# Bias-by-distance tiles: read back from DRAM rows written 128 times, in place of flips on TensorE

## Chip, cores and metric

The kernel runs on one core of a Trainium2 chip. The metric is the device time of one execution in microseconds. Before the change the median of three runs is 1805.74 us (1804.57 to 1810.54).

## The reference, cut to what matters

Two transformer blocks work one after the other on 256 tokens of width 1024. The first block has an attention over tokens and context (MLA), a Fourier mixer and a mixture of 32 experts. The second block has an "even" layer with two families of eight heads each (MoBA and NSA), an MLP, an "odd" layer with sixteen heads, and a second MLP. The change concerns the even layer alone, whose scores get a bias that depends on the head and on the distance of query and key:

```python
n = jnp.maximum(dist, 0)
large = 16 + (jnp.log(max(n, 1) / 16) / math.log(1024 / 16) * 16).astype(jnp.int32)
bucket = jnp.where(n < 16, n, jnp.minimum(large, 31))
s_own = einsum('hqd,hkd->hqk', q, k) * scale + rel_bias.T[:, bucket(t[:, None] - key[None, :])]
```

Keys after the query are masked. For each of the 16 heads the bias is therefore one row of numbers, a function of the distance, and the tile that the scores need is that row shifted by one place from each query to the next.

## The kernel before, in words

All large inputs come through one stream of chunks of at most 1 MB. `post_chunks`, `expert_chunks` and `pre_project` list them in the order of use. `Stream.pump` (line 152) issues the loads on SP's queue (line 164), in that order and as far ahead as ring buffers are free: ring A has 7 buffers, ring B 6, and rings C, D and E, opened one after the other before the experts, 3, 2 and 3. A job may carry other small loads behind its own (`also`, line 396). `Stream.prepare` (line 170) splits a chunk of float32 into a high and a low part (two ScalarE casts on line 1565, two VectorE subtractions on line 1566) in ring B, and `Stream.get` hands it to the matmuls.

Order of the stages: projections of the first block (`pre_project`), attention (`pre_attend`), output projection and routing (`pre_finish`), experts (`moe`), then `even`, `mlp`, `odd`, `mlp`. The output weights are four chunks ("o", in the order 3, 0, 1, 2; line 421) and right behind them in the stream come the expert weights, 384 chunks of 1 MB, and behind these the chunks of the second block.

The bias rows are made in these steps:

- `bias_rows_in` (line 1686) loads a table of 33 x 384 (a one-hot row per bucket, and the mask) on ScalarE's queue, at the end of `pre_attend`.
- `bias_rows` (line 1690) multiplies it by the 32 x 16 table of biases on TensorE, which gives 16 rows of 384 numbers, one per head. ScalarE evicts them with a factor of -1, and GpSimd's queue writes them to a DRAM tensor `scr` of 16 x 384. It runs in `pre_finish`, between two parts of the output projection.
- `bias_chunk2` (line 1699) adds two chunks to the stream, each of 1 MB: partition p of the chunk gets, for eight heads, the 256 numbers of the row from place p on. Two steps of one place, over partitions and over columns, can only shift in one direction, so the tile comes out with its queries upside down.
- `bias_tiles` (line 1706) turns it round: each chunk is split like a weight chunk and multiplied by a flipped unit matrix, in eight matmuls of 512 columns (four banks, high and low part), and ScalarE and VectorE evict the four banks in turn to the tile `bt[i]`.

`even_project` (line 1943) projects queries, keys and values in the order of the stream. The first tile is turned round after the second query chunk, ahead of the small matmul for the gates (line 2003); its bias is used first by the MoBA scores on line 1865. The second tile is turned round after the third pair of key chunks, ahead of the value projections; the NSA scores use it (line 2149). The small matmul for the gates needs its weights split by ScalarE and VectorE (`small_pair`, line 1821).

```python
for c in range(4):
    cols(w, 256 * c, None if c else self.split_first)
    if c == 1:
        self.bias_chunk2(0)
cols(w, 2048)
self.bias_chunk2(1)
```

Of the kernel before, what the change touches and what calls it, by code (L numbers as in the profile page):

```python
# [9 lines left out]
F32 = mybir.dt.float32  # L10
# [9 lines left out]
P = 128  # L20
D = 1024
KD = 8
T = 256
# [198 lines left out]
class Kernel:  # L222
# [142 lines left out]
    def pre_project(self, A, B):  # L365
# [8 lines left out]
        for nm, n in rows:  # L374
            src = I[nm]
            if len(src.shape) == 2:
# [21 lines left out]
                ("o", 3): self.expert_bias_in(B)}  # L398

        def add(nm, q, cols, f, split=None):  # L400
            st.add(cols, lambda v: f(v) + also.get((nm, q), []), 0, split)
# [62 lines left out]
        self.mrow = B.tile([P, 512], F32, name="mrow")  # L464
# [163 lines left out]
    def pre_attend(self, B, C):  # L628
# [66 lines left out]
        four_w()  # L695
        for h in range(6):
            b = self.bank()
            for k in range(2):
                self.mm3(b, [a[:, k, 256 * (h % 3) : 256 * (h % 3) + 128] for a in wkv[h // 3]], [a[:, k] for a in kvl], k == 0, k == 1)
            nc.vector.tensor_tensor(kn[:, h], b, rqk[:, 256:768], OP.mult)  # L700
            if h % 2 == 0:
                rope(qr[h // 2], 0, "q")
                split_rope(h // 2)
            if h in (2, 4):
                four_v(h // 2 - 1)
            self.modulation(MODS[h])
# [118 lines left out]
        self.bias_rows_in(B)  # L825
# [21 lines left out]
    def pre_finish(self, B, C, R):  # L847
# [15 lines left out]
        fills = [lambda: self.bcast_row(C, self.gc, g1b, bank="b"), router, lambda: self.bias_rows(B), lambda: self.down_bias_in(R),  # L863
# [730 lines left out]
    def post_chunks(self):  # L1594
# [21 lines left out]
        for c in range(4):  # L1616
            cols(w, 256 * c, None if c else self.split_first)
            if c == 1:
                self.bias_chunk2(0)
        cols(w, 2048)  # L1620
        self.bias_chunk2(1)
# [64 lines left out]
    def bias_rows_in(self, pool):  # L1686
        self.bk = pool.tile([E + 1, 384], F32, tag="mrow", name="bk")
        self.nc.scalar.dma_start(out=self.bk, in_=self.I["bucket"][0 : E + 1, 0:384])

    def bias_rows(self, pool):  # L1690

        nc, bk = self.nc, self.bk
        b = self.bank("bk", "s")
        nc.tensor.matmul(b[0:16, 0:384], self.rb, bk, start=True, stop=True)
        t = pool.tile([16, 384], F32, tag="krp", name="bkt")
        nc.scalar.mul(t, b[0:16, 0:384], -1.0)
        nc.gpsimd.dma_start(out=self.scr, in_=t)

    def bias_chunk2(self, i):

        def src(v):
            return [(v.rearrange("p (h c) -> p h c", h=8),
                     bass.AP(tensor=self.scr.tensor, offset=self.scr.offset + 8 * 384 * i, ap=[[1, P], [384, 8], [1, T]]))]
        self.stream.add((2048,), src, 0, self.split_plain)

    def bias_tiles(self, i, flip):

        nc = self.nc
        w = self.stream.get()
        for h in range(4):  # L1710
            b = self.bank("fl", "acc")
            for n in range(2):
                nc.tensor.matmul(b, flip, w[n][:, 512 * h : 512 * h + 512], start=(n == 0), stop=(n == 1))
            o = self.bt[i][:, 2 * h : 2 * h + 2].rearrange("p h c -> p (h c)")
            if h % 2:
                nc.vector.tensor_copy(o, b)
            else:
                nc.scalar.copy(o, b)
        self.stream.free()
# [223 lines left out]
    def even_project(self, W, X):  # L1943
# [4 lines left out]
        self.bt = [W.tile([P, 8, T], F32, tag=f"bt{i}", name="bt") for i in range(2)]  # L1948
        qk = W.tile([P, 16, T], F32, tag="qk", name="qk")
# [6 lines left out]
        flip = W.tile([P, 256], F32R, tag="hs1", name="flipr")[:, 0:P]  # L1956
        nc.scalar.copy(flip, self.c2("flip"))
# [42 lines left out]
        self.todo = []  # L2000
        self.bias_tiles(0, flip)
# [46 lines left out]
        self.bias_tiles(1, flip)  # L2048
# [393 lines left out]
def body(tc, I, out, dbg=None, upto=None):  # L2442
    nc = tc.nc
    K = Kernel(tc, I, dbg)
    with ExitStack() as es:
# [19 lines left out]
        K.scr = dr.tile([16, 384], F32, name="scr")[:]  # L2465
# [41 lines left out]
```

## Time and profile before

| What | Value |
|---|---|
| Median of three runs | 1805.74 us |
| The profiled execution | 1805.48 us |
| Its span, first to last instruction | 1803.7 us |
| TensorE busy | 1721.6 us (95%) |
| VectorE busy | 744.8 us (41%) |
| ScalarE busy | 583.3 us (32%) |
| Mean DMA rate over the span | 307 GB/s |
| Mean granted clock of TensorE | 0.996 |

The page cuts the span into 40 equal slices of 45.1 us. A busy share is an average over stages that have different limits, so the stages have to be looked at one by one: attention and routing end at some 200 us, the experts at some 1150 us, and the even layer follows. TensorE's busy time counts matmuls that overlap in the pipeline, and a busy TensorE need not be at its peak. DMA shares a little over 1 occur.

### The profile page before, as it was taken

The page shows a single profiled execution, that of the slowest core. Times are in us where ns is not written, and L with a number is a line of the kernel's source. Part 1 is how long each engine was busy: PE and PEld are TensorE (multiplying, and loading weights), DVE is VectorE, ACT ScalarE, POOL GpSimd, SP SyncE. Part 2 cuts the span into 40 slices and gives each one's busy share as a digit, 9 for nine tenths or more (in the row PEclk, how much of TensorE's full clock was granted, in tenths as well). Part 3 has the DMA queues.
Part 4 walks back from the last instruction along what each step waited for, and adds up shares of the span by engine and source line. Part 5 has one row for each costly group of instructions (what it writes and reads, how often), then busy time and mean ns, then how long its engine had stood idle before and what let it go on. Part 6 is the DMA issues. An engine that isn't in the chain of part 4 may idle for free.

```text
span 1803.7 us, 24461 instructions
## 1 busy us (share of the span) xinstructions
PE 1721.6 (95%) x9553; PEld 1031.0 (57%) x9553; DVE 744.8 (41%) x1604; ACT 583.3 (32%) x1147; POOL 22.8 (1%) x31
## 2 busy tenths in 40 slices
PE   8989999999999999999998998899999999999998
PEld 6756543333333333333332332588699989989997
DVE  4675522222221112212211112576665558756554
ACT  5534311111111111111111110555654446545444
POOL 0000000000000000000000000100000001000000
PEclk9999999999999999999999999999999999999999
DMA  9987899999999999999999999986165563345540
GB/s 351 327 278 278 322 386 410 411 412 412 412 412 411 411 412 412 413 412 411 411 412 413 413 413 412 312 241 189 48 210 187 187 186 129 131 139 196 185 147 24
DMA packets 202461, 553.45 MB, mean 307 GB/s; under 512 B 11136, under 2 KB 87430, under 8 KB 200294
## 3 DMA queue, kind: packets, MB, share of 16 engines
q1 hardware_dynamic: 201290, 550.35, 80.9%
q8 instruction: 76, 1.25, 0.3%
q0 software_dynamic: 576, 0.86, 0.2%
q10 hardware_dynamic: 476, 0.64, 0.1%
q14 instruction: 43, 0.35, 0.1%
HBM read 550.71 MB, written 1.07 MB: 306 GB/s over the span
## 4 chain that ended last, share of the span: by engine, by line
PE 72%; DMA 18%; DVE 6%; ACT 3%; issue 1%; SPq 0%; ACTq 0%; DVEq 0%
PE acc L1795 11%; PE g L1209 10%; PE u L1209 10%; PE ot L1780 10%; PE y L1220 8%; DMA ring<-in_w_gate 7%; DMA ring<-in_w_up 5%; DMA ring<-in_w_down 4%; PE pj L1780 4%; PE xg L1292 3%; PE pj L1787 2%; PE yb L1362 1%; PE bk L542 1%; PE mix L363 1%; DVE msum L314 1%
## 5 line engine op out<-in xcount | busy, mean ns | idle before, releaser
L1566 DVE TENSOR_TENSOR ring<-ring,ring 128x1024 fp32r<-128x1024 f32 (+1 forms) x200 | 234.3, 1215 | 77.8 <-ACT ring L1565 77.3
L1209 PE MATMUL g<-ring,xg 128*64 128x512 f32 x1056 | 254.9, 605 | 8.8 <-DMA ring<-in_w_gate 8.7
L1209 PE MATMUL u<-ring,xg 128*64 128x512 f32 x1056 | 248.2, 602 | 10.0 <-DMA ring<-in_w_up 9.2
L1220 PE MATMUL y<-ring,ht 128*64 128x512 f32 x1056 | 240.8, 598 | 16.2 <-DMA ring<-in_w_down 15.7
L1565 ACT CAST ring<-ring 128x1024 fp32r<-128x1024 f32 (+1 forms) x200 | 198.5, 1046 | 75.7 <-PE acc L1795 54.3
L1281 ACT ACTIVATE z<-y,gsl 64x512 fp32r<-64x512 f32 x66 | 45.0, 682 | 429.1 <-PE y L1220 402.1
L1780 PE MATMUL ot<-ahi,ring 128*128 128x256 f32 x960 | 177.2, 282 | 0.0
L1220 PEld LDWEIGHTS y<-ring,ht 128*64 128x64 f32 x1056 | 70.0, 136 | 164.7 <-issue 117.0
L1282 DVE SCALAR_TENSOR_TENSOR z<-y,gsl,z 64x512 fp32r<-64x512 f32 x66 | 49.5, 750 | 251.0 <-ACT z L1281 250.9
L1780 PEld LDWEIGHTS ot<-ahi,ring 128*128 128x128 f32 x960 | 151.3, 191 | 1.3
L1209 PEld LDWEIGHTS u<-ring,xg 128*64 128x64 f32 x1056 | 67.3, 136 | 131.9 <-issue 99.3
L1209 PEld LDWEIGHTS g<-ring,xg 128*64 128x64 f32 x1056 | 67.2, 137 | 128.6 <-issue 118.9
L1780 PE MATMUL ot<-alo,ring 128*128 128x256 f32 x480 | 135.6, 283 | 0.0
L1795 PE MATMUL acc<-ring,hhi 128*128 128x512 f32 x480 | 131.5, 395 | 0.0
L1795 PEld LDWEIGHTS acc<-ring,hhi 128*128 128x128 f32 x480 | 88.1, 188 | 19.0
L1228 ACT ACTIVATE sg<-gm 128x512 f32<-128x512 f32 x33 | 20.8, 630 | 239.5 <-DVE gm L1227 239.5
L1780 PEld LDWEIGHTS ot<-alo,ring 128*128 128x128 f32 x480 | 91.8, 191 | 1.3
L1294 ACT ACTIVATE xg<-xg,mod,a 128x128 f32<-128x128 f32 (+1 forms) x136 | 50.9, 452 | 99.2 <-PE xg L1292 99.2
L1292 PEld LDWEIGHTS xg<-pm,x 128*128 128x128 f32 x544 | 65.2, 195 | 26.8 <-issue 15.4
L1780 PE MATMUL pj<-ahi,ring 128*128 128x256 f32 x416 | 79.9, 287 | 0.0
L1271 DVE TENSOR_SCALAR gt<-gt,cp 128x256 fp32r<-128x256 f32 x33 | 16.0, 484 | 150.6 <-PE gt L1269 150.6
L1795 PE MATMUL acc<-ring,hlo 128*128 128x512 f32 x240 | 75.4, 395 | 0.0
(518 smaller groups left out, 2080.5 us busy)
## 6 DMA issues: line engine op xcount, KB each, us to landing
ring<-in_w_gate SPq DMA_DIRECT2D x128, 1024.0 KB, 17.9
ring<-in_w_up SPq DMA_DIRECT2D x128, 1024.0 KB, 17.9
ring<-in_w_down SPq DMA_DIRECT2D x128, 1024.0 KB, 17.9
ring<-in_mlp_w SPq DMA_DIRECT2D x64, 1024.0 KB, 5.4
ring<-in_w_mod SPq DMA_DIRECT2D x24, 1024.0 KB, 6.4
ring<-in_odd_w_in SPq DMA_DIRECT2D x12, 1024.0 KB, 5.3
ring<-in_even_w_in SPq DMA_DIRECT2D x7, 1024.0 KB
ring<-in_w_out SPq DMA_DIRECT2D x4, 1024.0 KB, 5.0
```

Source lines behind the costliest of these rows:

```text
L1209: nc.tensor.matmul(acc[64 * h : 64 * h + 64], xg[:, 2 * q + j], w[:, j, 512 * h : 512 * h + 512], start=(q == 0 and j == 0), stop=False, s ...
L1220: nc.tensor.matmul(acc[64 * h : 64 * h + 64], l, w[:, j, 512 * h : 512 * h + 512], start=(q == 0 and j == 0), stop=(q == 3 and j == 1), sk ...
L1228: nc.scalar.activation(sg, gm, AF.Sigmoid, scale=1.702)
L1281: nc.scalar.mul(t[s], a[s], g[s])
L1282: nc.vector.scalar_tensor_tensor(t[o], a[s], g[s], t[s].bitcast(F32), OP.mult, OP.subtract)
L1292: nc.tensor.matmul(b[:, n * j : n * j + n], self.x[:, t, (k + j) * P : (k + j + 1) * P], pm[:, t, 0:n], start=(t == 0), stop=(t == 1))
L1294: nc.scalar.activation(xg[:, k + j], b[:, n * j : n * j + n], AF.Identity, bias=self.mod[:, 0, 24 + k + j : 25 + k + j], scale=self.a2[:, ...
L1565: nc.scalar.copy(hi[:, c], v[:, c])
L1566: nc.vector.tensor_tensor(lo[:, c], v[:, c], hi[:, c].bitcast(F32), OP.subtract)
L1780: nc.tensor.matmul(out, w[a][:, k, c : c + n], x[b][:, k], start=(k == 0 and i == 0), stop=(k == KD - 1 and i == 2))
L1787: nc.tensor.matmul(out, x[a][:, k, t * P : (t + 1) * P], w[b][:, k, c : c + n], start=(k == 0 and i == 0), stop=(k == KD - 1 and i == 2))
L1795: nc.tensor.matmul(acc[2 * t + n], x[a][kx][:, t * P : (t + 1) * P], w[b][:, j, 512 * n : 512 * n + 512], start=(first and i == 0), stop=( ...
```

## The change

The row of each head is written to DRAM 128 times end to end (`scr` becomes 16 x 128 x 384). Read with a step of 383 from partition to partition, one less than the length of a row, it gives a tile whose rows shift the other way, so it comes out in the order that the scores want. The tile is read straight to `bt[i]`, in float32, with no split, no matmul and no eviction.

- The 33 x 384 table is loaded behind the second key/value chunk ("k", 1) on SP's queue. It lies in the buffer of `mrow`, which is allocated anew behind it.
- `bias_rows` runs in `pre_attend`, behind `four_w()`. Its result lies in a tile of its own, `bkt`.
- The two writes, heads 0 to 7 and heads 8 to 15, go on SP's queue with the job of output weights ("o", 1), the third of the four, behind its load.
- The two chunks of bias leave the stream.
- `bias_tiles(0)` issues its read on SP's queue at the start of `even_project`, `bias_tiles(1)` at the place where the second tile was turned round.

```diff
-                ("o", 3): self.expert_bias_in(B)}
+                ("k", 1): lambda: self.bias_rows_in(B), ("o", 3): self.expert_bias_in(B), ("o", 1): self.bias_rows_out}
 
         def add(nm, q, cols, f, split=None):
-            st.add(cols, lambda v: f(v) + also.get((nm, q), []), 0, split)
+            more = also.get((nm, q), [])
+            st.add(cols, lambda v: f(v) + (more() if callable(more) else more), 0, split)
...
-        self.mrow = B.tile([P, 512], F32, name="mrow")
+        self.mrow = B.tile([P, 512], F32, tag="mrow", name="mrow")
...
         four_w()
+        self.bias_rows(C)
+        self.mrow = B.tile([P, 512], F32, tag="mrow", name="mrow")
...
-        self.bias_rows_in(B)
...
-        fills = [lambda: self.bcast_row(C, self.gc, g1b, bank="b"), router, lambda: self.bias_rows(B), lambda: self.down_bias_in(R),
+        fills = [lambda: self.bcast_row(C, self.gc, g1b, bank="b"), router, lambda: None, lambda: self.down_bias_in(R),
...
             cols(w, 256 * c, None if c else self.split_first)
-            if c == 1:
-                self.bias_chunk2(0)
         cols(w, 2048)
-        self.bias_chunk2(1)
...
     def bias_rows_in(self, pool):
         self.bk = pool.tile([E + 1, 384], F32, tag="mrow", name="bk")
-        self.nc.scalar.dma_start(out=self.bk, in_=self.I["bucket"][0 : E + 1, 0:384])
+        return [(self.bk, self.I["bucket"][0 : E + 1, 0:384])]
 
     def bias_rows(self, pool):
 
-        nc, bk = self.nc, self.bk
+        nc = self.nc
+        self.bkt = pool.tile([16, 384], F32, name="bkt")
         b = self.bank("bk", "s")
-        nc.tensor.matmul(b[0:16, 0:384], self.rb, bk, start=True, stop=True)
-        t = pool.tile([16, 384], F32, tag="krp", name="bkt")
-        nc.scalar.mul(t, b[0:16, 0:384], -1.0)
-        nc.gpsimd.dma_start(out=self.scr, in_=t)
...
+        nc.tensor.matmul(b[0:16, 0:384], self.rb, self.bk, start=True, stop=True)
+        nc.scalar.mul(self.bkt, b[0:16, 0:384], -1.0)
+
+    def bias_rows_out(self):
+
+
+        return [(self.scr[8 * i : 8 * i + 8], self.bkt[8 * i : 8 * i + 8].unsqueeze(1).to_broadcast([8, P, 384])) for i in range(2)]
+
+    def bias_tiles(self, i):
+
+        s = self.scr
+        self.nc.sync.dma_start(out=self.bt[i], in_=bass.AP(tensor=s.tensor, offset=s.offset + 8 * P * 384 * i + P - 1, ap=[[383, P], [P * 384, 8], [1, T]]))
...
         self.bt = [W.tile([P, 8, T], F32, tag=f"bt{i}", name="bt") for i in range(2)]
+        self.bias_tiles(0)
...
-        flip = W.tile([P, 256], F32R, tag="hs1", name="flipr")[:, 0:P]
-        nc.scalar.copy(flip, self.c2("flip"))
...
-        self.todo = []
-        self.bias_tiles(0, flip)
...
-        self.bias_tiles(1, flip)
+        self.bias_tiles(1)
...
-        K.scr = dr.tile([16, 384], F32, name="scr")[:]
+        K.scr = dr.tile([16, P, 384], F32, name="scr")[:]
```

## Rows read from the trace of the kernel before

**Rows 1.** The page's part 2: DMA busy tenths and GB/s in 40 slices.

```profile
DMA  9987899999999999999999999986165563345540
GB/s 351 327 278 278 322 386 410 411 412 412 412 412 411 411 412 412 413 412 411 411 412 413 413 413 412 312 241 189 48 210 187 187 186 129 131 139 196 185 147 24
```

**Rows 2.** The page's part 5: busy us, mean ns | idle us before, its releaser.

```profile
L1209 PE MATMUL g<-ring,xg 128*64 128x512 f32 x1056 | 254.9, 605 | 8.8 <-DMA ring<-in_w_gate 8.7
L1209 PE MATMUL u<-ring,xg 128*64 128x512 f32 x1056 | 248.2, 602 | 10.0 <-DMA ring<-in_w_up 9.2
L1220 PE MATMUL y<-ring,ht 128*64 128x512 f32 x1056 | 240.8, 598 | 16.2 <-DMA ring<-in_w_down 15.7
```

**Rows 3.** Stretches: us; busy us (instructions) of five engines; clock; DMA share; GB/s.

```profile
120.00:250.00 130.00, 121.16 (x591) 75.46 (x592) 65.62 (x194) 45.54 (x98) 4.35 (x7) 0.96 0.84 309
...
155.00:180.00 25.00, 24.15 (x112) 18.35 (x111) 10.94 (x26) 10.37 (x19) 0.15 (x1) 1.00 1.02 398
...
250.00:1130.00 880.00, 845.28 (x3872) 308.41 (x3870) 181.85 (x378) 125.78 (x246) 0.00 (x0) 1.00 1.03 412
```

**Rows 4.** Timeline of TensorE: start us, us, engine, line, operation, count [idle before].

```profile
178.23 0.49 PE L1694 MATMUL bk<-bk,relb 33*16 33x384 f32 x1
...
203.50 2.88 PE L1209 MATMUL g<-ring,xg 128*64 128x512 f32 x8
...
1168.69 1.08 PE L1713 MATMUL fl<-ring,flipr 128*128 128x512 f32 x4
1170.69 1.28 PE L1713 MATMUL fl<-ring,flipr 128*128 128x512 f32 x4 [0.92 <-ACT bt L1718]
1171.81 1.10 PE L1836 MATMUL pj<-ahi,wz 128*64 128x256 f32 x8
...
1195.68 1.27 PE L1713 MATMUL fl<-ring,flipr 128*128 128x512 f32 x4
...
1199.22 0.40 PE L1787 MATMUL pj<-ring,ahi 128*128 128x256 f32 x2
```

**Rows 5.** Timeline of VectorE in the even layer.

```profile
1165.68 4.62 DVE L1566 TENSOR_TENSOR ring<-ring,ring 128x1024 fp32r<-128x1024 f32 x4
...
1170.43 0.42 DVE L1566 TENSOR_TENSOR wz<-wz 128x96 fp32r<-128x96 f32 x2
...
1185.98 0.28 DVE L1865 CUSTOM_DVE_ANT_0 p<-s,bt 128x128 f32<-128x128 f32 x1
...
1245.89 0.28 DVE L2149 CUSTOM_DVE_ANT_0 p<-s,bt 128x128 f32<-128x128 f32 x1
```

**Rows 6.** DMA issues: queue, count, KB each, median us from issue to landing.

```profile
ring<-scr SPq DMA_DIRECT2D x2, 1024.0 KB, 8.7
...
ring<-in_even_w_out SPq DMA_DIRECT2D x2, 1024.0 KB, 7.5
ring<-in_even_w_out SPq DMA_DIRECT2D x8, 256.0 KB, 8.6
...
bk<-in_bucket ACTq DMA_DIRECT2D x1, 49.5 KB
...
scr<-bkt POOLq DMA_DIRECT2D x1, 24.0 KB, 3.8
```

**Rows 7.** Timeline of SP's queue: start us, us from first issue to last.

```profile
112.56 5.85 SPq L164 DMA_DIRECT2D ring<-in_w_out  x3
...
1160.31 0.57 SPq L164 DMA_DIRECT2D ring<-scr  x1
...
1209.80 11.55 SPq L164 DMA_DIRECT2D ring<-in_even_w_out  x10
```

**Rows 8.** Stretches of the even layer, columns as in rows 3.

```profile
1213.00:1215.00 2.00, 2.00 (x21) 1.70 (x19) 0.00 (x0) 0.87 (x2) 0.00 (x0) 1.00 1.07 413
1221.00:1225.00 4.00, 4.00 (x45) 3.72 (x48) 1.88 (x6) 1.15 (x2) 0.00 (x0) 1.00 1.06 238
```

**Rows 9.** Timeline of ScalarE: the split of the last output-weight chunk.

```profile
161.97 1.99 ACT L1565 CAST ring<-ring 128x1024 fp32r<-128x1024 f32 x2 [1.86 <-PE mix L363]
```

More of the change, by code (lines that the diff above doesn't have):

```diff
@@ L1687, in bias_rows_in @@
         self.bk = pool.tile([E + 1, 384], F32, tag="mrow", name="bk")
-        self.nc.scalar.dma_start(out=self.bk, in_=self.I["bucket"][0 : E + 1, 0:384])
+        return [(self.bk, self.I["bucket"][0 : E + 1, 0:384])]
     def bias_rows(self, pool):
-        nc, bk = self.nc, self.bk
+        nc = self.nc
+        self.bkt = pool.tile([16, 384], F32, name="bkt")
         b = self.bank("bk", "s")
-        nc.tensor.matmul(b[0:16, 0:384], self.rb, bk, start=True, stop=True)
-        t = pool.tile([16, 384], F32, tag="krp", name="bkt")
-        nc.scalar.mul(t, b[0:16, 0:384], -1.0)
-        nc.gpsimd.dma_start(out=self.scr, in_=t)
[L1699 to L1719, printed above, removed]
+        nc.tensor.matmul(b[0:16, 0:384], self.rb, self.bk, start=True, stop=True)
[5 more added lines that the diff above has]
+        self.nc.sync.dma_start(out=self.bt[i], in_=bass.AP(tensor=s.tensor, offset=s.offset + 8 * P * 384 * i + P - 1, ap=[[383, P], [P * 384, 8], [1, T]]))
     def turn_x(self, W, gcol):
```

## The prediction

> **What bounds the kernel now.** I read the page first, its slices of time above all: from the seventh slice to the 25th the DMA engines are busy throughout and move some 412 GB/s, before and after that they do not [rows 1]. The costliest groups next: the three matmul groups of the experts stand idle for 8.7, 10.0 and 16.2 us, nearly all of it for weight chunks that have not landed [rows 2]. So the experts run at the pace of the DMA stream, with TensorE close behind. Then the stretches: from 250 to 1130 us the mean is 412 GB/s at a DMA share of 1.03, so not one chunk can be caught up there; from 120 to 250 us it is 309 GB/s, because SP waits for ring buffers [rows 3]. The stream therefore has free room of 130 x (1 - 309/412) = 32 us ahead of the saturated stretch, and none in it. Whatever is put into the stream at 120 us costs nothing up to about 32 us, and the whole excess over that comes out at the end of the experts. After the experts TensorE is the bound: in the even layer it runs matmul behind matmul, and the flips stand in that row [rows 4].
>
> The profiled execution took 1805.48 us for a span of 1803.7; the median of the runs is 1805.74. I work from 1805.5.
>
> **What goes away on TensorE.** The flips of the first half begin at 1168.69, and the gates' matmul behind them at 1171.81. But that matmul also needs the split gate weights, and VectorE finishes them only at 1170.43 + 0.42 = 1170.85, after four splits of 4.62 us [rows 4, 5]. The splits ahead of it are as many afterwards, since the next chunk moves up in place of the bias chunk. So the first flips give back 1171.81 - 1170.85 = 1.0 us, not 3.1. The flips of the second half begin at 1195.68 and the next projection at 1199.22 with nothing else in between; its weights were split one chunk earlier now, so all 3.5 us come back. Together 4.5 us. The bounds are 3.0 (the work behind meets VectorE a little later) and 3.1 + 3.5 = 6.6 (VectorE, which has four splits and four copies less in the even layer, no longer holds the gates).
>
> **Small edits, together zero.** The bias row's matmul moves from between the output projection's parts, where it starts at 178.23 [rows 4], to a place ahead of attention; it costs the same there and neither place is in the saturated stretch: at most 0.5 us either way. The load of the bucket table, 33 rows of 1.5 KB, goes from ACT's queue to SP's: 50 KB are 0.1 us at 412 GB/s. GpSimd loses one DMA of 24 KB [rows 6]. Reading the tiles back moves the same 2 x 1 MB in the same 1 KB pieces as the two ring loads that it replaces, which landed in 8.7 us [rows 6]; the first tile is asked for at about 1160 us, where SP now issues the second ring load, and first read at 1185.98, so 17 us of cover remain [rows 5, 7]. The second is asked for at about 1196 and read only in the second family of heads, from 1245.89 on [rows 5]. SP waits for the tiles' memory before it issues each, and the even layer's ring loads queue behind; those feed a TensorE that waits for no load there, so zero. If that cover went, the tile would be waited for in the first scores.
>
> **What is added.** Two writes of 8 x 128 x 384 x 4 bytes, 3.15 MB together where 24 KB went before. They sit in SP's queue right behind the third output-weight load, issued between 112.56 and 118.4 us, and everything behind them is what the experts need: the last output-weight chunk, then all expert weights [rows 7]. They wait for the evicted bias row, which is there some 20 us earlier, so the wait itself holds nobody up. The source is eight partitions each time. The trace has no such transfer, so I bound it. From below: at the stream's full rate, 3.15 MB / 412 GB/s = 7.6 us. From above by the row that shows what few partitions do: loads of 256 KB to 64 partitions ran at 238 GB/s, with a DMA share of 1.06, so all engines were busy and each slow; the 1 MB loads of the same tensor, to all 128 partitions, ran just before at 413 [rows 6 to 8]. Half the partitions, 0.58 of the rate. In strict proportion to the partitions eight of them get 238 x 8/64 = 30 GB/s, and the writes last 105 us. The ends are far apart. The 64-partition row is the one nearest in kind, since it alone shows partitions and not bytes setting the rate; but it fell by less than half, and I take the rate to go on falling by 0.58 at each halving: 413 x 0.58^4 = 47 GB/s for eight, which makes 67 us. That holds if stores behave as loads do, so I shade it a little towards the lower end and take **57 us**, 55 GB/s.
>
> [...]
>
> **The sum.** The writes last 57 us from about 120 us, so the chunks behind them land from 177 us on. Of this 57 - 32 = 25 us do not fit the room. The last output-weight chunk is late too: its split sits in ScalarE's and VectorE's queues at 161.97 [rows 9], and all their work behind it, the last heads' evictions and the broadcast of the attention gain, waits to about 180. The bias row's tile is freed with attention's buffers, and whatever is put in its place waits until the writes have read it, no longer than that. That delays TensorE's first expert matmul, now at 203.50 [rows 4], by some 15 us, inside the 25 and not on top of them, because the expert chunks land later still. From there the stream runs at 412 GB/s to the end of the experts, 25 us late. 1805.5 + 25 - 4.5 = **1826 us**.
>
> **Rivals.**
> - *The writes fit the room, and the kernel is faster.* For it: a store reads SBUF, it does not write it, and the halved rate was seen in loads only; the room of 32 us is over four times the 7.6 us at full rate. It decides at 32 us, that is at 98 GB/s, 1.8 times my rate. Then only the flips are left: 1805.5 - 4.5 = 1801. The last output-weight chunk may then be as late as 160 us without touching its split. Against it: the even layer's rows, where all engines were busy and still slow. [...] The chance is 0.26.
> - *Partitions count in full proportion.* 105 us of writes, 73 beyond the room, 1805.5 + 73 - 4.5 = 1874. For it: half the partitions came near half the rate. Against it: not quite. The chance is 0.08.
> - *The excess and the flips cancel.* Writes of 32 to 42 us: within about 5 us of before. The chance is 0.06.
> - *The change doesn't do what it says* (the tiles not read from the new rows): the reads replace the ring loads in number and size, and no step is left that could make the tiles otherwise; below 0.01.
>
> **How the numbers follow.** The forecast, writes of 42 to 80 us, has 0.60; its own range is 1811 to 1849, with 1826 as the value. What a measurement can tell from no change is about 0.3%, 5.4 us. Faster by more needs the writes hidden and the flips worth over 5.4 us, in the upper part of their bounds, 3.0 to 6.6; ScalarE and VectorE each have four splits and four copies less there, which speaks for that part. So the faster rival's 0.26 splits into 0.15 beyond 0.3% and 0.11 within. Faster 0.15, same 0.11 + 0.06 = 0.17, slower 0.60 + 0.08 = 0.68. The range takes in the forecast's core and the faster rival: 1799 to 1838; left out are the proportional case, 0.08, and the slow end of the forecast, about 0.1.
>
> **What would show it.** Right: a hole or slow stretch in GB/s from about 120 to 177 us at a high DMA share; the first expert matmul at about 218; the last matmul of the experts some 25 us late; the small gates' matmul straight behind the second projection's last matmul with some 2 us of waiting for VectorE; no flips at the second place. Wrong: if the stretch from 155 to 180 us still moves close to 398 GB/s [rows 3], the writes were short, and the time is about 1801. If ScalarE's split of the last output chunk still starts near 162, its load was not held up. If the first score of the even layer waits for a load, the read-back is not covered, and I have left a cost out.

## The result and the profile after

| | before | after |
|---|---|---|
| median of the runs | 1808.14 us (4 runs, 1804.57 to 1812.72) | 1834.14 us (4 runs, 1832.39 to 1835.38) |
| ratio after / before, 95% interval | | 1.0142 [1.0114, 1.0170] |
| profiled execution: time, span | 1805.48, 1803.7 us | 1832.39, 1830.6 us |
| mean granted clock of TensorE | 0.996 | 0.986 |
| start of the experts' last down projection | 1144.04 us | 1175.17 us |
| from there to the end of the span | 659.7 us | 655.4 us |
| written to HBM | 1.07 MB | 4.19 MB |

The kernel is slower by 26.0 us at the median, against 20.5 us forecast. The two rows on the last down projection split the 26.9 us between the two profiled spans in the way the prediction did: 31.1 us are lost up to the end of the experts, 4.2 us come back behind them.

The page's part 2 of the kernel after, DMA busy tenths and GB/s in 40 slices of the span, is to be read against [rows 1]:

```profile
DMA  9875999999999999999999999896255564435540
GB/s 350 315 229 112 361 400 413 413 412 411 410 411 413 412 413 409 411 411 412 412 410 412 413 408 411 324 280 208 70 169 188 189 186 144 138 115 200 186 156 24
```

From the sixth slice to the end of the experts the two kernels look alike. The third and fourth slices, some 92 to 183 us, hold 229 and 112 GB/s where there were 278 and 278. The stretches, with the columns of [rows 3] (us; busy us of the five engines; granted clock; DMA share; GB/s):

```profile
120.00:250.00 130.00, 96.47 (x461) 63.51 (x461) 58.78 (x175) 42.09 (x91) 3.92 (x6) 0.87 0.79 251
130.00:140.00 10.00, 7.38 (x28) 4.03 (x27) 6.34 (x14) 2.29 (x6) 0.00 (x0) 0.84 0.44 58
140.00:150.00 10.00, 9.27 (x37) 5.25 (x35) 5.78 (x12) 4.77 (x9) 0.00 (x0) 0.90 0.44 60
155.00:180.00 25.00, 16.99 (x82) 13.58 (x80) 9.88 (x20) 6.44 (x11) 0.00 (x0) 0.92 0.62 126
180.00:215.00 35.00, 17.84 (x77) 13.83 (x78) 9.18 (x20) 7.60 (x14) 2.09 (x4) 0.71 0.94 340
250.00:1130.00 880.00, 843.76 (x3888) 310.77 (x3889) 181.94 (x383) 126.15 (x250) 0.00 (x0) 1.00 1.02 411
```

The first 10 us that lie wholly in the writes, 130 to 140, read in the kernel before:

```profile
130.00:140.00 10.00, 6.65 (x25) 3.08 (x24) 6.58 (x16) 3.90 (x8) 0.00 (x0) 1.00 0.53 197
```

The kernel after moves 58 GB/s there at a share of 0.44, against 197 at 0.53. So it isn't one load among others that got slow: the slow writes are there and nearly nothing else, and they keep busy what seven of sixteen engines would be. The trace's DMA packets say so too. The writes are 2048 packets of 1536 bytes, which run from 124.7 to 189.0 us; they make 47 of the 58 GB/s from 130 to 140 us and all of the 60 from 140 to 150. The stretch from 155 to 180 us, named in the prediction as the one that decides, moves 126 GB/s where it moved 398. From 250 us on the stream runs at 411 GB/s, as before: nothing is caught up there.

The timeline of SP's queue (start, us from the first issue to the last) shows the loads standing behind the writes; [rows 7] has 5.85 us for three output-weight chunks. The 114.12 row is the second and third chunk:

```profile
114.12 4.12 SPq L164 DMA_DIRECT2D ring<-in_w_out  x2
118.48 20.63 SPq L164 DMA_DIRECT2D scr<-bkt  x2
139.22 23.34 SPq L164 DMA_DIRECT2D ring<-in_w_out  x1
162.65 21.84 SPq L164 DMA_DIRECT2D ring<-in_w_gate  x4
```

Issuing the two writes takes SP 20.63 us, the one output-weight chunk behind them 23.34 us and four gate chunks 21.84 us. The kernel before issues its first four gate chunks over 23.62 us, from 118.50 on, but nearly all of that is time between the issues: the four issuing instructions take 3.0 us there and 21.6 in the kernel after, and the first of them goes out 44 us later. ScalarE's split of that output chunk, in its timeline, waits 27.64 us for it and starts at 191.99 instead of 161.97 [rows 9]:

```profile
191.99 1.99 ACT L1567 CAST ring<-ring 128x1024 fp32r<-128x1024 f32 x2 [27.64 <-DMA ring<-in_w_out]
```

TensorE's first expert matmul starts at 230.06 instead of 203.50 [rows 4], and the last down projection, in TensorE's timeline of before and after, at 1175.17 instead of 1144.04:

```profile
230.06 1.94 PE L1211 MATMUL g<-ring,xg 128*64 128x512 f32 x8
```

```profile
1144.04 1.94 PE L1220 MATMUL y<-ring,ht 128*64 128x512 f32 x8 [0.69 <-DMA ring<-in_w_down]
```

```profile
1175.17 1.94 PE L1222 MATMUL y<-ring,ht 128*64 128x512 f32 x8 [0.65 <-DMA ring<-in_w_down]
```

The missing bytes fit that. Between 120 and 250 us the DMA engines moved 130 x (309 - 251) = 7.5 MB less than before, and 3.15 MB of what they moved were the writes: the load stream was behind by 10.7 MB, which at 412 GB/s are 26 us. In TensorE's timeline the experts' down projections are 25.6 us late from the first one (272.7 against 247.1) to the one at 544.5, then 32.4 us late by the one at 605.3 (572.8 before), and 31.1 at the last. So the experts do not simply hand on a fixed lag: some 6 us more appear about a third of the way through them. No run separates these.

Behind the experts the flips are gone. TensorE's timeline at the first place, to be read against [rows 4]:

```profile
1198.72 2.03 PE L1759 MATMUL pj<-ahi,ring 128*128 128x256 f32 x16
1202.09 1.15 PE L1822 MATMUL pj<-ahi,wz 128*64 128x256 f32 x8 [1.33 <-DVE wz L1568]
...
1205.18 0.38 PE L1766 MATMUL pj<-ahi,ring 128*128 128x256 f32 x1
```

The gates' matmul stands right behind the second projection and waits 1.33 us for the split gate weights, which VectorE's timeline has at this time (compare the split in [rows 5]):

```profile
1201.78 0.42 DVE L1568 TENSOR_TENSOR wz<-wz 128x96 fp32r<-128x96 f32 x2
```

### The profile page after: what moved, and what is told of

Read it like the earlier page. It is cut to its first block, busy times and chain, and to the rows that moved or that the text cites. A ratio compares the mean times of both kernels' runs of the same rounds, so it can differ in the third digit from the quotient of the medians.

```text
span 1830.6 us, 24413 instructions
## 1 busy us (share of the span) xinstructions
PE 1722.7 (94%) x9537; PEld 1029.7 (56%) x9537; DVE 737.2 (40%) x1596; ACT 577.6 (32%) x1138; POOL 22.4 (1%) x30
## 3 DMA queue, kind: packets, MB, share of 16 engines
HBM read 550.71 MB, written 4.19 MB: 303 GB/s over the span
## 5 line engine op out<-in xcount | busy, mean ns | idle before, releaser
L1568 DVE TENSOR_TENSOR ring<-ring,ring 128x1024 fp32r<-128x1024 f32 (+1 forms) x196 | 229.7, 1216 | 105.0 <-ACT ring L1567 104.4
L1567 ACT CAST ring<-ring 128x1024 fp32r<-128x1024 f32 (+1 forms) x196 | 194.6, 1046 | 103.4 <-PE acc L1781 54.0
```

Of the source, the lines that this page charges most:

```text
L1567: nc.scalar.copy(hi[:, c], v[:, c])
L1568: nc.vector.tensor_tensor(lo[:, c], v[:, c], hi[:, c].bitcast(F32), OP.subtract)
```

## The experiments

Theory: eight neighbouring partitions hold each other up, the two writes run at some 50 GB/s whatever the rest does, and while they run the load stream stands. Its free room of 32 us before the experts absorbs the first part; the rest appears at the experts' end. The rivals: it is the number of partitions or of DMA engines and not which partitions; the late output chunk stalls the attention stage; the read-back or the missing flips cost something; one stop of the queue costs a fixed time.

All runs in one table. "2 x 8 neighbours" means two writes, each from eight neighbouring partitions. "Last down" is the start of the experts' last down projection in the profiled execution, "rest" the span less that. Each ratio is against the kernel before on the same chip; the medians come from several chips, on which that of the kernel before lies between 1806.2 and 1809.9 us, so kernels are compared by their ratios.

| kernel | rows in DRAM written from | median us (runs) | ratio [95%] | last down | rest |
|---|---|---|---|---|---|
| before | one copy, late | 1808.1 (4) | 1 | 1144.0 | 659.7 |
| after | 2 x 8 neighbours | 1834.1 (4) | 1.0142 [1.0114, 1.0170] | 1175.2 | 655.4 |
| e1_spread | 128 partitions | 1807.9 (12) | 1.0003 [0.9991, 1.0015] | 1145.9 | 655.0 |
| e2_apart | 2 x 8, four apart | 1804.7 (10) | 0.9978 [0.9965, 0.9991] | 1147.7 | 655.2 |
| e4_later | 2 x 8 neighbours, one chunk later | 1835.6 (4) | 1.0144 [1.0126, 1.0162] | 1181.0 | 655.2 |
| e5_writes_flips | 2 x 8 neighbours, flips kept | 1837.5 (4) | 1.0157 [1.0139, 1.0174] | 1179.2 | 659.5 |
| e9_spread_pool | 128 partitions | 1802.0 (12) | 0.9962 [0.9948, 0.9976] | 1146.4 | 654.7 |
| e10_apart_pool | 2 x 8, four apart | 1801.0 (12) | 0.9964 [0.9950, 0.9977] | 1141.8 | 654.9 |
| e8_copies32 | 2 x 8 neighbours, 32 copies | 1800.5 (9) | 0.9959 [0.9944, 0.9973] | 1143.0 | 655.1 |
| e6_double | 4 x 8 neighbours | 1892.2 (4) | 1.0458 [1.0428, 1.0489] | 1231.4 | 657.8 |
| e11_rows_early | one copy, early, flips kept | 1805.3 (11) | 0.9974 [0.9961, 0.9987] | 1146.1 | 659.4 |
| e3_one16 | 1 x 16 neighbours | 1800.6 (6) | 0.9957 [0.9943, 0.9971] | 1144.2 | 654.7 |
| e12_spread_again | 128 partitions | 1807.8 (12) | 0.9996 [0.9984, 1.0008] | 1149.8 | 655.1 |
| e13_before_again | one copy, late | 1807.4 (10) | 1.0003 [0.9991, 1.0016] | 1146.3 | 659.3 |

### e1_spread: the same bytes from 128 partitions

```diff
-        self.bkt = pool.tile([16, 384], F32, name="bkt")
+        self.bkt = pool.tile([P, 384], F32, name="bkt")
+        r8 = pool.tile([E + 1, 16, 8], F32, name="rb8")
+        nc.vector.tensor_copy(r8, self.rb.unsqueeze(2).to_broadcast([E + 1, 16, 8]))
...
-        return [(self.scr[8 * i : 8 * i + 8], self.bkt[8 * i : 8 * i + 8].unsqueeze(1).to_broadcast([8, P, 384])) for i in range(2)]
+        return [(self.scr.rearrange("h (c j) n -> (h c) j n", c=8), self.bkt.unsqueeze(1).to_broadcast([P, 16, 384]))]
```

> The bias rows are made in 128 partitions (each head's row eight times, by eight equal columns in the table) and written by one transfer from all of them; bytes in DRAM are the same 3.15 MB, in the same place of the queue. My theory, that eight neighbouring partitions set the 65 us of the writes: at the stream's rate they take about 8 us, well inside the room of 32, the last output-weight chunk is split near 162 again, and only the flips' gain is left, 1801 us (1799 to 1804). Rival, that 3.15 MB of writes in pieces of 1.5 KB are slow from any source: still about 1834. Rival, that the place in the queue matters and not the length: some 10 us above the forecast, 1811.

The excess is gone, with the same 3.15 MB to write: the last down projection starts at 1145.9. The stretches of this kernel move 310 and 307 GB/s:

```profile
120.00:155.00 35.00, 27.74 (x122) 15.96 (x121) 24.02 (x57) 11.64 (x27) 0.00 (x0) 0.95 0.88 310
155.00:180.00 25.00, 24.02 (x112) 18.45 (x110) 15.52 (x36) 14.54 (x26) 2.09 (x4) 1.00 0.80 307
```

But the time comes out level with before, not below it, though the rest behind the experts is 4.7 us shorter. One suspect is an addition of mine, in TensorE's timeline:

```profile
85.26 1.53 PE L1696 MATMUL bk<-bk,rb 33*128 33x384 f32 x2 [2.66 <-issue]
```

The little copy of the bias table stands in VectorE's queue behind other work, and TensorE waits 2.66 us for it. VectorE's timeline has the copy at that time:

```profile
84.94 0.22 DVE L1694 COPY rb<-relb 33x128 f32<-33x128 f32 x1
```

The kernel after has no such wait. What follows on the wait is in the stretches 85 to 90 and 90 to 95 us of this kernel:

```profile
85.00:90.00 5.00, 4.74 (x11) 3.03 (x11) 0.40 (x2) 0.49 (x1) 0.00 (x0) 0.53 0.62 261
90.00:95.00 5.00, 5.00 (x22) 3.12 (x21) 3.16 (x7) 3.16 (x6) 0.00 (x0) 0.78 0.12 20
```

The granted clock falls to 0.53 in the mean, and the load stream falls to 20 GB/s: SP's longest wait there for a ring buffer that TensorE's matmuls hold is 11.3 us, against 5.5 in e9_spread_pool. e9, e10 and e12 look into this.

### e2_apart: eight partitions still, but four apart

```diff
+        self.bkt = pool.tile([64, 384], F32, name="bkt")
+        r4 = pool.tile([E + 1, 16, 4], F32, name="rb4")
+        nc.vector.tensor_copy(r4, self.rb.unsqueeze(2).to_broadcast([E + 1, 16, 4]))
...
-        return [(self.scr[8 * i : 8 * i + 8], self.bkt[8 * i : 8 * i + 8].unsqueeze(1).to_broadcast([8, P, 384])) for i in range(2)]
+        return [(self.scr[8 * i : 8 * i + 8], self.bkt[32 * i : 32 * i + 32 : 4].unsqueeze(1).to_broadcast([8, P, 384])) for i in range(2)]
```

> Still two transfers of eight rows from eight partitions each, but the partitions lie four apart (0, 4, 8 and so on) and not side by side. Theory, that neighbouring partitions share a way out of the memory: every row has its own, the rate rises from 48 GB/s several times, to between 150 and 200, the writes take 16 to 21 us, inside the room: 1801 us (1799 to 1805). Rival, that a transfer of eight rows is slow because few engines carry it, or because eight partitions are few wherever they lie: 48 GB/s again and 1834 us.

Two writes of eight rows each, as in the change, with nothing altered but which partitions the rows lie in (and the small copy that puts them there), and the excess is gone: 386 GB/s from 155 to 180 us against 126, a ratio of 0.9978 against 1.0142. So neither "eight partitions" nor "few engines" is the reason; that the partitions are neighbours is. How many neighbours hold each other up, this run doesn't tell: four apart is far enough. This kernel has the same 2.6 us wait for VectorE's copy as e1_spread.

### e4_later: the writes behind the last output-weight chunk

```diff
-                ("k", 1): lambda: self.bias_rows_in(B), ("o", 3): self.expert_bias_in(B), ("o", 1): self.bias_rows_out}
+                ("k", 1): lambda: self.bias_rows_in(B), ("o", 3): self.expert_bias_in(B), ("o", 2): self.bias_rows_out}
```

> The two writes as in the change, but behind the fourth output-weight chunk and not ahead of it. Theory, that the excess of the writes over the stream's room is what costs: the expert weights are as late as before and the time stays near 1834 (1828 to 1838), although ScalarE's split of the fourth chunk is back near 162 and TensorE's idle 24.6 us ahead of the expert stage go. Rival, that the stall behind the late output chunk is the cost: 1801 to 1808.

ScalarE's timeline shows the last output chunk split without a wait for its load (168.18, against 161.97 before and 191.99 in the change), and TensorE's the first expert matmul no earlier for that:

```profile
168.18 1.99 ACT L1567 CAST ring<-ring 128x1024 fp32r<-128x1024 f32 x2 [1.85 <-PE mix L363]
```

```profile
231.50 1.94 PE L1211 MATMUL g<-ring,xg 128*64 128x512 f32 x8
```

The time is that of the change. So the attention stage's late chunk, 191.99 in the kernel after, is a symptom; the experts' own weights are late by as much, whichever chunk stands behind the writes.

### e5_writes_flips: the writes of the change, the tiles read as before

```diff
+            if c == 1:
+                self.bias_chunk2(0)
...
+        self.bias_tiles(0, flip)
...
-        self.bias_tiles(1)
+        self.bias_tiles(1, flip)
```

> The change without its second half: the bias rows are made and written 128 times as in the change, but the tiles come through the ring and are turned round on TensorE as before. Theory: the writes alone cost some 31 us at the end of the experts and the flips keep their 4.5, so 1805.7 + 31 = 1837 (1833 to 1841), 3 to 6 above the change. Rival, that the read-back straight to the tiles costs something itself: below the change, 1830 or less.

```profile
1179.15 1.94 PE L1222 MATMUL y<-ring,ht 128*64 128x512 f32 x8 [0.70 <-DMA ring<-in_w_down]
```

The rest from that row of TensorE's timeline to the end is 659.5 us, as in the kernel before (659.7), against 655.4 in the kernel after. The loss belongs to the writes alone, and the read-back with its missing flips gives 4.1 us.

### e9_spread_pool and e10_apart_pool: without my wait for VectorE

```diff
-        nc.vector.tensor_copy(r8, self.rb.unsqueeze(2).to_broadcast([E + 1, 16, 8]))
+        nc.gpsimd.tensor_copy(r8, self.rb.unsqueeze(2).to_broadcast([E + 1, 16, 8]))
```

e10_apart_pool has the same edit on r4 of e2_apart.

> The spread rows (128 partitions, one write) with the 33x128 copy of the small table made by the idle GpSimd in place of VectorE. In e1_spread that copy stood behind VectorE's work, TensorE waited 2.66 us for it at 82.6 us, and the granted clock then read 0.53 from 85 to 90 us. Theory: this wait ate what the even layer gave back. Then TensorE's idle time before the bias matmul is below 0.6 us, the clock from 80 to 95 us is 1.00, the first output-projection load is issued at 108 to 111 us (114.2 in e1_spread), and the time is that of before less the 4.6 us that the even layer gave back in the change: about 1804, ratio 0.9965 to 0.9985. Rival (the spread write itself costs what the even layer gives): about 1808 again, ratio 0.999 to 1.001, though the wait is gone.

> Two writes of eight rows from partitions 4 apart, as in e2_apart, with the copy of the small table made by GpSimd. Same theory: the wait of 2.63 us before the bias matmul and the half clock after it go, and the time falls from 1804.7 by some 2 to 4 us, to 1801 to 1803 (ratio 0.996 to 0.997). Rival (that wait cost nothing, since the expert stage is bound by transfers and the load stream has room before it): 1804 to 1806, as e2_apart.

Both are below the kernel before by 6.5 to 7 us going by the ratio; e9_spread_pool's 0.9962 is a little lower than the 0.9965 to 0.9985 expected. The same two stretches of e9_spread_pool show the clock at full speed and the stream running:

```profile
85.00:90.00 5.00, 5.00 (x27) 2.99 (x27) 3.26 (x9) 0.49 (x1) 0.00 (x0) 1.00 0.75 269
90.00:95.00 5.00, 5.00 (x26) 3.25 (x25) 3.98 (x9) 3.29 (x6) 0.00 (x0) 1.00 0.84 311
```

One step of the expectation failed: the first output-projection load went out at 113.08 us, not at 108 to 111. In the profiled executions that time wanders between 107.7 and 117.2 without the end following it, so it is no measure of what the wait cost; and the spans of the two profiled executions, 1800.9 and 1801.1, don't show the difference either (e1_spread's was the fastest of its 12 runs). It rests on the timed runs, and e12_spread_again repeats them.

The stretches of e10_apart_pool while its writes run:

```profile
130.00:140.00 10.00, 6.78 (x22) 2.76 (x20) 6.34 (x14) 2.45 (x8) 0.00 (x0) 0.83 0.47 177
140.00:150.00 10.00, 9.87 (x47) 7.26 (x48) 7.58 (x16) 4.85 (x10) 0.00 (x0) 1.00 0.97 372
```

At 130 to 140 us the share is 0.47, about eight engines of sixteen, at 177 GB/s, of which the writes' packets make 174. About as many engines, 0.44, move 58 GB/s in the kernel after. What separates the two is the partitions: a packet of 1536 bytes takes 0.065 us in the mean here and 0.187 us in the kernel after. The writes run from 123.1 to 146.7 us, 24 us where the change's took 64.

### e8_copies32: a quarter of the copies

```diff
-        return [(self.scr[8 * i : 8 * i + 8], self.bkt[8 * i : 8 * i + 8].unsqueeze(1).to_broadcast([8, P, 384])) for i in range(2)]
+        return [(self.scr[8 * i : 8 * i + 8], self.bkt[8 * i : 8 * i + 8].unsqueeze(1).to_broadcast([8, 32, 384])) for i in range(2)]
...
+        for a in range(0, P, 32):
+            self.nc.sync.dma_start(out=self.bt[i][a : a + 32], in_=bass.AP(tensor=s.tensor, offset=s.offset + 8 * 32 * 384 * i + P - 1 - a, ap=[[383, 32], [32 * 384, 8], [1, T]]))
```

> The change with 32 copies of a row in place of 128, from the same eight neighbouring partitions, and each tile read back by four DMAs of 32 partitions, each from an offset 32 less. Theory (eight neighbouring partitions give 48 GB/s, and the load stream has some 32 us of room before the experts): the writes last 65/4 = 16 us, fit into the room, and the time is that of before less the even layer's 4.6 us, 1802 to 1806. Rival 1 (a write from few partitions has a cost that does not shrink with the bytes, such as the stop of the load queue behind it): 1820 or more. Rival 2 (four DMAs of 32 partitions each are late for the tiles): the even layer gives back nothing, 1808 to 1812.

The change's own slow source, a quarter of its bytes, and the kernel is faster than before by 0.41%, at 1800.5 us even below the 1802 to 1806 expected. The writes' packets run from 124.4 to 137.2 us, 13 us. The scratch is 16 x 32 x 384 here. The cost does shrink with the bytes, down to nothing once they fit the room: the last down projection starts at

```profile
1142.99 1.94 PE L1222 MATMUL y<-ring,ht 128*64 128x512 f32 x8 [0.68 <-DMA ring<-in_w_down]
```

which is 1.1 us ahead of the kernel before. Eight reads of 256 KB in place of two of 1 MB, in the page's part 6, keep nobody waiting; the rest is 655.1 us as elsewhere:

```profile
bt<-scr SPq DMA_DIRECT2D x8, 256.0 KB
```

### e6_double: the writes twice

```diff
-        return [(self.scr[8 * i : 8 * i + 8], self.bkt[8 * i : 8 * i + 8].unsqueeze(1).to_broadcast([8, P, 384])) for i in range(2)]
+        return [(s[8 * i : 8 * i + 8], self.bkt[8 * i : 8 * i + 8].unsqueeze(1).to_broadcast([8, P, 384])) for s in (self.scr, self.scr2) for i in range(2)]
...
+        K.scr2 = dr.tile([16, P, 384], F32, name="scr2")[:]
```

This kernel writes a second set of rows that nothing reads.

> The change with the two writes issued twice, the second pair to another scratch, 6.3 MB in all. Theory (the writes hold 48 GB/s, other loads get 60 to 70 GB/s beside them, and the room before the experts is used up by the first pair): 65 us more of slow writes, in which the loads lose 65 x (1 - 65/412) = 55 us and at most 65 us: 1887 to 1900. Rival (the cost is that of one stop, such as TensorE's late start or a reordered queue): 1834 to 1845.

The median rises by 58 us over the change, and the last down projection, in TensorE's timeline, by 56.2:

```profile
1231.36 1.94 PE L1222 MATMUL y<-ring,ht 128*64 128x512 f32 x8 [0.66 <-DMA ring<-in_w_down]
```

So past the room the second pair of writes costs its full duration. The writes by themselves are in the stretch from 180 to 215 us, where TensorE and all others have run dry:

```profile
180.00:215.00 35.00, 0.00 (x0) 0.00 (x0) 0.00 (x0) 0.00 (x0) 0.00 (x0) 0.50 0.41 57
```

57 GB/s, at a share of 0.41. At that rate a pair of 3.15 MB takes 55 us, about what the second pair costs. The rest, 657.8 us, is 2.4 above the other kernels without flips; I leave that open.

### e3_one16: one write from 16 neighbouring partitions

```diff
-        return [(self.scr[8 * i : 8 * i + 8], self.bkt[8 * i : 8 * i + 8].unsqueeze(1).to_broadcast([8, P, 384])) for i in range(2)]
+        return [(self.scr, self.bkt.unsqueeze(1).to_broadcast([16, P, 384]))]
```

> The change with one write from 16 neighbouring partitions in place of two from 8, the same 3.1 MB. [...] Rival (a write that is cut into sixteen is spread over all the engines, and engines alone set the rate): 8 to 15 us of writes, 1800 to 1803, and 120 to 155 us at over 300 GB/s. Third (the two writes of the change already ran at the same time on eight partitions' ways each, so nothing is won): 1830 or more.

The DMA issues of this kernel (KB, median us from issue to landing), then its stretches:

```profile
scr<-bkt SPq DMA_DIRECT2D x1, 3072.0 KB, 37.8
```

```profile
130.00:140.00 10.00, 7.09 (x30) 3.58 (x28) 6.34 (x14) 2.48 (x7) 0.00 (x0) 1.00 0.88 109
155.00:180.00 25.00, 24.02 (x114) 19.11 (x113) 14.84 (x31) 10.59 (x19) 2.09 (x4) 1.00 1.01 396
180.00:215.00 35.00, 33.19 (x193) 22.56 (x191) 18.09 (x79) 15.56 (x37) 1.83 (x2) 1.00 1.02 399
```

109 GB/s from 130 to 140 us, of which the write's own packets make 95, twice the 47 of eight neighbours in the same stretch, at a share of 0.88 where those had 0.44. Over its whole length, from 125.2 to 156.1 us, the write moves 102 GB/s, against 49 for the pair. So nearly all engines are busy and the rate is still a quarter of the stream's; the rival of engines alone falls, though its time, 1800 to 1803, fits. The write lands 37.8 us after its issue (31 us after its first packet), and the stretches show where the room was: 396 and 399 GB/s from 155 to 215 us, where the kernel before had 398 and 301. The stream stands during most of the 35 us ahead of that, makes it up before the experts need the chunks, and the last down projection starts at 1144.2, as in the kernel before. With one line altered this is the change as it should have been: ratio 0.9957.

### e11_rows_early: of the change, only the moved making of the rows

```diff
-        return [(self.scr[8 * i : 8 * i + 8], self.bkt[8 * i : 8 * i + 8].unsqueeze(1).to_broadcast([8, P, 384])) for i in range(2)]
+        return [(self.scr, self.bkt)]
```

The diff is against e5_writes_flips; the scratch is back to [16, 384], and the two chunks read it by the old addresses. Against the kernel before, the row matmul's place has moved, and the table's load and the 24 KB write have moved to SP's queue.

> The rows are made where the change makes them and leave in one write of 24 KB at the change's place in the load queue, but without copies; the tiles come through the ring and the flip matmuls as in the kernel before. Of the change only the moved making of the rows is left. In e8_copies32, e9 and e10 the median fell by 7 to 9 us, of which the stretch behind the experts gives 4.7. Theory A (the rest comes from making the rows early, off the stage behind the output projection): 1804 to 1806, ratio 0.9975 to 0.999, with 659.5 us from the last down projection to the end, as before. Theory B (the rest is the spread of the runs, and the place of the rows is worth nothing): 1808 to 1810, ratio 0.9985 to 1.0015.

Theory A, at 0.9974 just below its 0.9975 to 0.999: making the rows early, with its two small transfers, is worth 4.5 us at the median. Where it comes from no profile shows. The profiled execution, 1807.24 us, is the slowest of this kernel's 11 runs, its last down projection at

```profile
1146.13 1.94 PE L1222 MATMUL y<-ring,ht 128*64 128x512 f32 x8 [0.75 <-DMA ring<-in_w_down]
```

and its rest of 659.4 us is that of the kernel before. What is seen is that this kernel has no run above 1807.24 us, where over half of the runs of the kernel before on this chip lie above 1808 (median 1809.85, up to 1814.13). The granted clock of the single runs goes with this: in the 25 runs of the kernel before it falls from 0.998 (1800.97 us) to 0.991 (1814.13 us), some 1.5 us for each 0.001; its mean is 0.9927 there and 0.9949 in the 11 runs of this kernel, which would go with 3.4 of the 4.4 us between the mean times. Whether the clock is the cause, or only shows that TensorE stood still for longer, no run decides.

### e12_spread_again and e13_before_again

e12_spread_again is e1_spread without an edit, e13_before_again the kernel before.

> e1_spread once more, with its VectorE copy ahead of the bias matmul, on the chip of this call. Theory (the stall of TensorE at 82 us and the half clock after it cost 4 to 6 us): ratio 0.999 to 1.0015 again, above e9_spread_pool's interval (0.9948 to 0.9976). Rival (the two differed by their chips or by chance): ratio 0.995 to 0.998.

The first theory: 0.9996, clear of e9's interval, so the stall of 2.7 us at TensorE costs 6 to 7 us at the median with the spread rows (0.9996 and 1.0003 against 0.9962, times 1808 us). With the rows four apart it is 2.5 us (e2_apart's 0.9978 against 0.9964 in e10_apart_pool), with intervals that overlap. Each pair differs only in the engine of the small copy. Here too the mean granted clock of the runs goes with the time: 0.9912 in e1_spread and 0.9918 in e12_spread_again, 0.9938 in e9_spread_pool.

> The kernel before once more, unchanged, for a second profiled execution: the first one (1803.7 us) lies at the lower end of its runs (1801 to 1814 us), and making the rows early took 4.5 us off the median without showing in a profile. [...]

Inconclusive: the profiled execution took 1807.36 us, so none of the runs above 1808 us is in a profile. It has its last down projection at 1146.3, 2.2 us later than the first profile, and the same rest, so these 1.9 us arise ahead of the experts' end; that is too little to say what the runs of 1810 us and more do.

## Why the prediction was right, point by point

**What it said and what came.** It forecast 1826 with a chance of 0.68 for slower; 1834.14 came, inside 1799 to 1838. The mechanism holds in each of its links: the DMA stream bounds the experts (rows of after as [rows 2], [rows 3]), it has a room ahead of them and none inside, writes from eight neighbouring partitions overfill it, and the even layer gives a few microseconds back.

**The writes: the term that was mis-sized.** The prediction took 57 us, or 55 GB/s. Alone the writes move 57 GB/s (e6_double from 180 to 215 us), so the rate was right. But the trace has their packets from 124.7 to 189.0 us, 64 us, 49 GB/s in the mean: 59 up to 160 us, and 37 from there on, where other loads run beside them. In place of 57 - 32 = 25 us of excess the experts' end came 31.1 us later in the profile. By the medians it is 33: e3_one16, which differs from the change in the write alone and hides it, has 0.9957, the change 1.0142, and 0.0185 x 1808 = 33. That is close to 64 - 32. What the prediction scaled with 0.58 for each halving of the partitions, 47 GB/s for eight, and then shaded towards the faster end, was better unshaded as the mean rate; the step from 67 to 57 us had no row behind it. As a law it is wrong all the same: at 16 neighbours it would give 413 x 0.58^3 = 81 GB/s, and 95 to 102 were measured; and eight partitions four apart are not slow at all.

What the runs show is that neighbours hold each other up: two writes from eight neighbouring partitions ran at 57 GB/s alone and 49 over their whole length, one from sixteen at 95 to 102, and with the same count of partitions four apart the excess is gone (e2_apart). What holds them up, and how many neighbours hold each other up, no run shows.

**The room.** 32 us of it were worked out from 309 against 412 GB/s [rows 3]. e3_one16's write, 31 us by its packets, cost nothing at the experts' end; e6_double, with the room used up, paid 56 to 58 us for its second 3.15 MB. Between these the change pays 31 to 33 for 64 us of writes, which leaves 31 to 33 for the room.

**The first expert matmul: 218 forecast, 230.06 measured.** The step that failed is the output chunk's arrival at about 180: it is split at 191.99. The chunk lands as the writes end, as forecast; but they began at 124.7 and not at about 120, and lasted 64 us and not 57, so that they ended 12 us later than the forecast's 177, and these 12 us are the whole miss. This stayed inside the excess, as forecast, and e4_later shows it costs nothing by itself.

**The even layer: right.** 4.5 us forecast with bounds 3.0 and 6.6; the rest shrank by 4.2 us between the two profiles and is 4.5 to 5.0 us shorter than before in eight other kernels without flips, e6_double alone apart. The wait for VectorE at the gates, 1.33 us against the "some 2 us" forecast, and no flips at the second place, as told. The read-back is covered, but less well than forecast: it is asked for at 1199.5 and first read at 1214.7, 15 us later and not 26 (1160 to 1185.98), and with a landing of 7.6 us, as e4_later has it, some 8 us of cover are left against 17. The medians give less, 0.9974 to 0.9957 or 3 us, with intervals that overlap.

**The small edits: wrong.** They were costed at zero, at most 0.5 us either way. e11_rows_early measures 4.5 us of gain (0.1 to 0.4%) for making the rows ahead of attention. The prediction looked at the bias matmul's own 0.49 us [rows 4] and at one execution from the lower end of the runs, and took a place in an unsaturated stretch for a free one. What it is worth there isn't visible in a single profile, so the cause stays open.

The parts, by ratios: -4.7 (rows early) - 3.1 (read-back) + 33 (writes) = +25, against +25.7 for the change. They are the differences along one chain of kernels, from the kernel before by e11_rows_early and e3_one16 to the change, so that they add up is no test. Set beside the forecast they show some luck: it had 0, -4.5 and +25. The writes were priced 8 us too low and the read-back 1.4 us too high, and the 4.7 us that it put at nothing took back half of that. Without these 4.7 us the time would have been some 1839, just outside the range.

**The rivals.** "The writes fit the room" was right about what decides, 98 GB/s, and wrong about the change; e3_one16 at 102 GB/s lies on its side of that line, just, and its cost is hidden. That its 1800.6 is the 1801 that the rival gave is chance: on that chip the kernel before has 1809.85, and the rows made early are part of the gain. Of the engines the runs show shares of 0.41 to 0.47 for the eight-row writes, where these run nearly alone, and 0.88 for the sixteen-row one, but that share does not set the time: in e10_apart_pool, at 0.47, the pair's packets take 24 us, beside other loads, at 174 GB/s from 130 to 140 us, and in the kernel after, at 0.44, 64 us. "In full proportion", 30 GB/s, is refuted by 57.

## What to carry to other kernels

Ask of each transfer which partitions its SBUF side touches, and price it by neighbours (measured here: 49 to 57 GB/s for eight that lie side by side, 95 to 102 for sixteen, 174 for eight that lie four apart); a small table spread over the partitions, or one DMA in place of two halves one after the other, can be the whole difference between +1.4% and -0.4%. A slow transfer in the queue that feeds a saturated stage cost its duration here, not its bytes, less the free room ahead of that stage (64 less 32 us; nothing for the 31 us of e3_one16); read the room from GB/s by stretch, and if the bytes are copies, look for an access pattern that needs fewer (32 copies and four reads did here). And a feeder matmul should have its operands long before its turn: 2.7 us of waiting cost 2.5 us in one pair of kernels and over 6 in the other.

## What was not expected of the hardware

- In e1_spread a pause of 2.66 us of TensorE at 82 us is followed by a granted clock of 0.53 from 85 to 90 us, and the loads fall to 20 GB/s from 90 to 95 us, as ring buffers come free late. The cost at the median, 2.5 us in one pair of kernels and 6 to 7 in the other, is up to twice the pause and more, in a stage that has room in its load stream.
- While the slow writes run, other loads don't merely share: with over half of the DMA engines' time free (a share of 0.44), the queue's loads moved nothing from 140 to 150 us (60 GB/s in all, every packet of them the writes'), though SP had been issuing a load since 139.22. SP's instruction for that chunk took 23.34 us and those for the next four 21.6, where three chunks had taken 5.85. Whether the writes in another queue would leave the stream alone wasn't tried.
- The form of the write matters as much as its size: the same bytes as one write from 16 neighbours ran at 102 GB/s, as two from 8 at 49. The one write took SP only 1.59 us to issue where the pair took 20.63, but the chunk behind it then took 18.80 us, so the queue was held up all the same.
